# Activations stationary in the gated branch and the convolution input of an encoder trunk

## The chip, the cores and the metric

The kernel runs on one core of a Trainium2 chip. The metric is the device time of one execution in microseconds, the median of several runs. The engines named below are TensorE (PE; its weight loads are listed as PEld), VectorE (DVE), ScalarE (ACT), GpSimd (POOL) and the DMA queue of SyncE (SP). A matmul takes a stationary operand (128 x 128, loaded first) and streams a moving operand past it; the result goes to PSUM, whose banks hold 512 float32 columns on 128 partitions.

## What is computed

Two pre-norm residual layers over 256 tokens of width 2048 (float32). Layer 0 mixes tokens by neighbourhood attention, layer 1 by a gated short convolution; both end in a gated MLP with a convolution of three taps over the tokens, and a last norm closes the trunk.

```python
def short_conv_mixer(x, w_in, conv_w, w_out):
    gb, gc, h = jnp.split(x @ w_in, 3, axis=-1)          # 2048 -> 3 x 2048
    return (gb * dwconv_centered(gc * h, conv_w)) @ w_out

def conv_glu_ffn(x, w_up, conv_w, conv_b, w_down):       # 2048 -> 2 x 5632 -> 2048
    h = dwconv_centered(x @ w_up, conv_w) + conv_b
    g, u = jnp.split(h, 2, axis=-1)
    return (jax.nn.silu(g) * u) @ w_down

h = x
for i in range(2):
    a = rms_norm(h, mix_norm[i])
    h = h + (neighborhood_attention(a, ...) if i == 0 else short_conv_mixer(a, ...))
    h = h + conv_glu_ffn(rms_norm(h, ffn_norm[i]), ...)
return rms_norm(h, final_norm)
```

## The kernel before

Every float32 operand is split in two parts of the type fp32r, a rounded one (hi) and the rest (lo). A product is the sum of three: hi by hi, hi by lo, lo by hi. `split` and `scaled_split` do this for activations, `parts` for weights (ScalarE rounds, VectorE subtracts, L118 and L119).

Weights are streamed once, in chunks of 512 KB. `prep_to` loads them on the SP queue into `raw` (five buffers) and splits them into `hi` and `lo` (six each); it runs AHEAD = 4 chunks in front of the matmuls. Chunks of kind "rows" are one output tile by eight input tiles, 4 KB a partition; chunks of kind "cols" are four output tiles by two input tiles, four pieces of 1 KB a partition.

All work is a list `items`, one for each chunk, run in order by the loop at the end of `trunk`. What has to follow an item is put off with `after(n, fn)`: it is issued n items later. That list is the order of the program on every engine as far as the operands allow.

There are three kinds of product:

- **Phase** keeps a weight tile stationary and streams the activations (`a`, hi and lo side by side, 512 columns; then the lo weight against the hi activations, 256 columns, L156 and L157). Its result has channels on the partitions and tokens along the columns. `normed` adds the two halves and multiplies by `rstd` of each token, `conv` applies the taps to a padded tile in SBUF (L206 to L211), and the gate follows. Phase serves query and key (`wqk`), both halves of the gated branch (`wup`) and the convolution input (`wsc`).
- **Values** keeps the activations stationary (L474 to L476).
- **Tokens** keeps the activations stationary too, and streams the weights, 512 columns at a time, three matmuls for hi-hi, hi-lo and lo-hi (L304 to L306). Its result has tokens on the partitions, which the residual stream `h` needs. Two column blocks of 512 by two token tiles occupy the four `pm` banks. It serves the output projection, the down products and the convolution output. For the input pairs listed in `S_DOWN` and `S_OUT` the four blocks are computed by seven products instead of eight, from sums of blocks (`seven`, `sums`, `make_forms`), with four more banks (tags st, sc, tr, o).

A down half has 22 input tiles (11 pairs) and 2048 outputs; an up half has 44 output tiles. After each Tokens product that ends a mixer or an MLP, `to_norm` squares the new residual, transposes it back (L245) and scales it to the next `a`; `token_rstd` computes one over the root mean square, as a column `rcol` and spread over the partitions as `rstd` (L257).

Of the kernel before, what the change touches and what calls it, by code (L numbers as in the profile page):

```python
# [21 lines left out]
P = 128  # L23
# [11 lines left out]
CH = 8  # L35
AHEAD = 4

S_DOWN = (2, 5, 8)
S_OUT = (1, 3, 5)
# [12 lines left out]
def trunk(ctx, tc, xT, par, bias, wqk, wv, wo, wsc, wscout, wup, wdown, out):  # L52
# [12 lines left out]
    acc = cp.tile([P, S], F32, name="acc")  # L65
    NPAD = 3
    pads = [cp.tile([P, S + 2], F32, name=f"pad{i}") for i in range(NPAD)]
    pad_at = [0]

    def next_pad():  # L70
        pad_at[0] += 1
        return pads[pad_at[0] % NPAD]

# [7 lines left out]
    for p_ in pads:  # L81
        nc.gpsimd.memset(p_[:, 0:S + 2:S + 1], 0.0)
# [39 lines left out]
    def sums(l, r):  # L122

        t13 = wp.tile([P, CH * P], F32, name="raw", tag="raw", bufs=5)
# [70 lines left out]
    def normed(dst, ps):  # L195

        corr = tp.tile([P, S], F32, name="corr", tag="corr", bufs=3)
# [4 lines left out]
    def conv(x, w, b):  # L202

        c = tp.tile([P, S], F32, name="conv", tag="conv", bufs=4)
        if b is None:
            nc.scalar.activation(c, x[:, 1:S + 1], AF.Copy, scale=w[1])  # L206
        else:
            nc.scalar.activation(c, x[:, 1:S + 1], AF.Identity, scale=w[1], bias=b)  # L208
        for tap in (0, 2):
            nc.vector.scalar_tensor_tensor(out=c, in0=x[:, tap:tap + S], scalar=w[tap], in1=c,  # L210
                                           op0=ALU.mult, op1=ALU.add)  # L211
        return c
# [10 lines left out]
    def stats(sums):  # L223
# [4 lines left out]
        v = tp.tile([P, S], F32, name="v", tag="v", bufs=1)  # L228
        rt = tp.tile([P, 2, S], F32, name="rt", tag="s")
        rsqrt(rstd, v, rt[:, 0, :], rt[:, 1, :], ps)  # L230

    def residual(t, q, ps):
        x = h[:, t, q * 4 * P:(q + 1) * 4 * P]
        nc.vector.tensor_add(out=x, in0=ps, in1=x)

    def squares(t, q, ssq):
        nc.scalar.activation(tp.tile([P, 4 * P], F32, name="s", tag="s"), h[:, t, q * 4 * P:(q + 1) * 4 * P],
# [10 lines left out]
    def token_rstd(ssq):  # L248
# [3 lines left out]
        rsqrt(rcol, v, tp.tile([P, 2], F32, name="m", tag="m"), tp.tile([P, 2], F32, name="m", tag="m"), v)  # L252
        diag = tp.tile([P, S], F32, name="conv", tag="conv", bufs=4)
# [6 lines left out]
    class Tokens:  # L260
# [3 lines left out]
        def __init__(self, parts, src, evac, sset=(), forms=None):  # L264

            self.src, self.evac, self.sset, self.forms = src, evac, sset, forms
            self.nk = sum(n for _, n in parts)
            for g in range(KT // 8):
                base = 0
                for w, n in parts:  # L270
                    for k0 in range(0, n, 2):
                        k = base + k0
                        left, right = (w[f:f + 4, :, k0 * P:(k0 + 2) * P] for f in (8 * g, 8 * g + 4))
                        c = len(chunks)
                        chunks.append((left, 8 * P, "cols"))
                        if k // 2 in sset:
                            chunks.append((right, 8 * P, "sums"))
                            items.append((self, g, c + 1, k, k, k + 2))
                        else:
                            chunks.append((right, 8 * P, "cols"))  # L280
                            items.append((self, g, c, k, k, k + 2))
                            items.append((self, g, c + 1, k, k, k + 2))
                    base += n

        def run(self, g, c, k0, ka, kb):
            if k0 // 2 in self.sset:
                return self.seven(g, c, k0)
            hi, lo, _ = prepped[c]
            right = len(prepped[c - 1]) == 3 and (self, g, c - 1, k0, ka, kb) in items[at[0] - 1:at[0]]
            if not right and ka == 0:  # L290
                self.c = {n: pm.tile([P, 4 * P], F32, name="mm", tag="mm") for n in ("11", "21", "12", "22")}
                self.begun = set()
            for t in range(2):
                ps = self.c["12"[t] + "12"[right]]
# [5 lines left out]
                if kb == self.nk:  # L300
                    self.evac(t, 2 * g + right, ps)
# [6 lines left out]
        def seven(self, g, c, k0):  # L308
            i = k0 // 2
            first, last = i == min(self.sset), i == max(self.sset)  # L310
            if first:
                self.u = [pa.tile([P, 4 * P], F32, name="mu", tag=n) for n in ("st", "sc", "tr", "o")]
            a, e, f, b = self.u
# [4 lines left out]
            for ps, x, w, j in ((a, raw(0, 0), left, 0), (self.c["11"], raw(1, 0), left, 1), (self.c["12"], s4, w22, 0),  # L318
                                (e, s1, t13, 0), (f, s3, t13, 1), (b, s2, t24, 0), (self.c["21"], raw(1, 1), t24, 1)):
                own = ps in self.u  # L320
                self.product(ps, *x, *(y[:, j * 4 * P:(j + 1) * 4 * P] for y in w[:2]), own and first, own and last)
            if last:
                after(1, lambda: self.combine(g))

        def combine(self, g):

            a, e, f, b = self.u
            sa, u = (tp.tile([P, 4 * P], F32, name="s", tag="s") for _ in range(2))
            o = {(t, n): h[:, t, (2 * g + n) * 4 * P:(2 * g + n + 1) * 4 * P] for t in range(2) for n in range(2)}
# [8 lines left out]
            nc.vector.tensor_add(out=o[1, 0], in0=o[1, 0], in1=u)  # L338

    form_at = [0]  # L340

    def make_forms(xe, xo):

        n = form_at[0] = (form_at[0] + 1) % 3
        y = tp.tile([P, 8 * P], F32R, name="sf", tag="vv" if n else "sf", bufs=2 if n else 1)
        v = tp.tile([P, 4, P], F32, name="s", tag="s")
# [10 lines left out]
    def to_norm(n, a):  # L357
# [3 lines left out]
        def evac(t, q, ps):  # L361
            residual(t, q, ps)
            squares(t, q, ssq)

            def next_input():
                for k0, tag in zip(range(4 * q - 4, 4 * q + 4, 2), ("tr", "o", "sc", "st")):
                    tr = transposed(k0, tag)
                    for k in range(2):
                        a[k0 + k] = a_tile()
                        scaled_split(a[k0 + k], tr[:, k, :], norm_g(n, k0 + k))  # L370
            if t and q % 2:
                after(1, next_input)
                if q == KT // 4 - 1:
                    after(2, lambda: nc.vector.tensor_copy(rstd, token_rstd(ssq)))
        return evac
# [10 lines left out]
    def qk_evac(f, ps):  # L386
# [8 lines left out]
        if which == 0:  # L395
            b = tp.tile([P, 6 * GRID_W], F32, name="bias", tag="bias")
# [8 lines left out]
    def scores(h):  # L405
# [8 lines left out]
        s = tp.tile([P, 2, S], F32, name="s", tag="s")  # L414
# [80 lines left out]
    def sc_evac(f, ps):  # L495
        j, which = divmod(f, 3)
        w = [pt[:, C_SC + 3 * j + i:C_SC + 3 * j + i + 1] for i in range(3)]
        tag, bufs = ("conv", 4) if which else ("g", 2)
        t = tp.tile([P, S], F32, name="scx", tag=tag, bufs=bufs)
        normed(t, ps)  # L500
        if which == 0:
            sc_of["gc"] = t
        elif which == 1:
            pad = next_pad()
            nc.vector.tensor_mul(out=pad[:, 1:S + 1], in0=sc_of["gc"], in1=t)
            sc_of["c"] = conv(pad, w, None)
        else:
            nc.vector.tensor_mul(out=t, in0=t, in1=sc_of["c"])
            yT[j] = act_tile()
            split(yT[j], t)  # L510
            if j % 2 == 0:
                sc_of["even"] = t
            elif j // 2 in S_OUT:
                yforms[j // 2] = make_forms(sc_of["even"], t)
# [4 lines left out]
    def up_evac(layer, act, forms):  # L519
        def evac(f, ps):  # L520
            j, which = divmod(f, 2)
            ft = j + which * FT
            w = [pt[:, C_CW + (layer * 2 * FT + ft) * 3 + i:C_CW + (layer * 2 * FT + ft) * 3 + i + 1] for i in range(3)]
            b = pt[:, C_CB + layer * 2 * FT + ft:C_CB + layer * 2 * FT + ft + 1]
            pad = next_pad()
            normed(pad[:, 1:S + 1], ps)
            c = conv(pad, w, b)
            if which == 0:
                g = tp.tile([P, S], F32, name="g", tag="g")
                nc.scalar.activation(g, c, AF.Silu)  # L530
                glu["g"] = g
            else:
                nc.vector.tensor_mul(out=c, in0=c, in1=glu["g"])  # L533
# [4 lines left out]
                elif j % HALF // 2 in S_DOWN:  # L538
                    forms[j % HALF // 2] = make_forms(glu["even"], c)
# [3 lines left out]
    def last_evac():  # L543
# [3 lines left out]
        def evac(t, q, ps):  # L547
            residual(t, q, ps)
            squares(t, q, ssq)
# [159 lines left out]
```

## Time and profile before

| What | us |
|---|---|
| Median of 3 runs (2243.35 to 2248.56) | 2244.75 |
| The profiled execution's own time | 2248.17 |
| Its span, from the first instruction to the last | 2246.4 |
| VectorE busy | 1740.8 |
| ScalarE busy | 1216.9 |

The mean granted TensorE clock was 0.997 of full speed. Every group of lines is listed with its busy time and the mean duration of one instruction; for TensorE these durations overlap, so that the distance between starts, in the timeline, is what one costs. Idle time of an engine is listed with what ended it. The other lines stand in the prediction, where they are used.

### The profile page before, as it was taken

To read this page: it belongs to the slowest core of one execution; us is meant where nothing else is said; L and a number is where in the kernel's file an instruction comes from. 1 tells how busy PE (TensorE), PEld (TensorE's weight loads), DVE (VectorE), ACT (ScalarE), POOL (GpSimd) and SP (SyncE) were. 2 spreads that over 40 slices of the span, in tenths; PEclk is the share of its full clock that TensorE was granted. 3 is DMA by queue.
4 is the path that set the end of the run, shared out by engine and by line. 5 is a ranking of instruction groups with operands and counts; after the bars stand their busy time and mean duration, and the time that the engine had idled before them with its cause. 6 is when DMAs were issued, how large, how long until landed. Compare 5 with 4: busy or idle time off the path is not lost.

```text
span 2246.4 us, 31725 instructions
## 1 busy us (share of the span) xinstructions
PE 2226.4 (99%) x11818; PEld 1902.9 (85%) x11818; DVE 1740.8 (77%) x2546; ACT 1216.9 (54%) x1822; POOL 85.0 (4%) x110
## 2 busy tenths in 40 slices
PE   8999999999999999999999999999999999999997
PEld 6888888888888888888888888888888888888886
DVE  7777665687887778887877777898888778887876
ACT  5555554655554555555554444566555545555553
POOL 3111000000000000000000000000000000000000
PEclk9999999999999999999999999999999999999998
DMA  7565555555556655555665565565555666555563
GB/s 239 177 190 173 183 171 189 178 187 188 185 172 192 217 190 188 188 183 174 191 211 188 188 190 185 171 221 187 190 189 187 180 203 207 187 186 185 166 193 125
DMA packets 209689, 420.97 MB, mean 187 GB/s; under 512 B 13312, under 2 KB 136192, under 8 KB 209536
## 3 DMA queue, kind: packets, MB, share of 16 engines
q1 hardware_dynamic: 207792, 414.72, 58.0%
q0 software_dynamic: 1024, 3.15, 0.5%
q8 instruction: 93, 1.52, 0.3%
q10 hardware_dynamic: 720, 1.09, 0.1%
q14 instruction: 60, 0.49, 0.1%
HBM read 416.81 MB, written 2.10 MB: 186 GB/s over the span
## 4 chain that ended last, share of the span: by engine, by line
PE 98%; DVE 1%; issue 0%; ACT 0%; DVEq 0%
PE mm L156 42%; PE mm L157 21%; PE mm L304 8%; PE mm L306 8%; PE mm L305 8%; PE mm L474 1%; PE mm L475 1%; PE mm L476 1%; PE mu L305 1%; PE mu L304 1%; PE mu L306 1%; PE tr L245 1%; PE tr L436 0%; DVE a L573 0%; PE sc L412 0%
## 5 line engine op out<-in xcount | busy, mean ns | idle before, releaser
L156 PE MATMUL mm<-a,hi 128*128 128x512 f32 x4096 | 1445.3, 398 | 4.4 <-DVE a L186 3.2
L119 DVE TENSOR_TENSOR lo<-raw,hi 128x1024 fp32r<-128x1024 f32 (+1 forms) x820 | 988.8, 1213 | 392.6 <-ACT hi L118 388.7
L118 ACT CAST hi<-raw 128x1024 fp32r<-128x1024 f32 (+1 forms) x820 | 840.3, 1029 | 825.2 <-issue 465.0
L157 PE MATMUL mm<-a,lo 128*128 128x256 f32 x4096 | 1145.9, 280 | 0.8 <-DVE lo L119 0.8
L156 PEld LDWEIGHTS mm<-a,hi 128*128 128x128 f32 x4096 | 770.3, 188 | 192.3 <-DVE a L186 6.1
L157 PEld LDWEIGHTS mm<-a,lo 128*128 128x128 f32 x4096 | 773.7, 189 | 3.5 <-DVE lo L119 2.3
L304 PE MATMUL mm<-hi,act 128*128 128x512 f32 x780 | 304.6, 391 | 0.0
L306 PE MATMUL mm<-hi,act 128*128 128x512 f32 x780 | 304.1, 390 | 0.0
L305 PE MATMUL mm<-lo,act 128*128 128x512 f32 x780 | 303.5, 389 | 0.0
L210 DVE SCALAR_TENSOR_TENSOR conv<-pad,pt,conv 128x256 f32<-128x256 f32 x384 | 184.6, 481 | 10.9 <-ACT conv L208 3.9
L306 PEld LDWEIGHTS mm<-hi,act 128*128 128x128 f32 x780 | 146.4, 188 | 31.3
L305 PEld LDWEIGHTS mm<-lo,act 128*128 128x128 f32 x780 | 146.5, 188 | 30.5
L304 PEld LDWEIGHTS mm<-hi,act 128*128 128x128 f32 x780 | 146.4, 188 | 30.4
L208 ACT ACTIVATE conv<-pad,pt 128x256 f32<-128x256 f32 x176 | 105.4, 599 | 15.3 <-DVE pad L200 14.3
L199 DVE TENSOR_TENSOR corr<-mm,corr 128x256 f32<-128x256 f32 x256 | 106.4, 416 | 0.0
L198 ACT COPY corr<-mm 128x256 f32<-128x256 f32 x256 | 92.4, 362 | 0.4 <-PE mm L157 0.3
L200 DVE TENSOR_TENSOR pad<-corr,rstd 128x256 f32<-128x256 f32 x176 | 74.9, 426 | 5.6
L119 DVE TENSOR_TENSOR lo<-t,hi 128x1024 fp32r<-128x1024 f32 x30 | 36.7, 1224 | 22.9 <-ACT hi L118 22.8
L351 POOL TENSOR_TENSOR s<-conv 128x128 f32<-128x128 f32 x12 | 5.5, 461 | 1265.6 <-DVE conv L533 948.9
L474 PE MATMUL mm<-hi,a 128*128 128x512 f32 x128 | 50.7, 396 | 0.0
L118 ACT CAST hi<-t 128x1024 fp32r<-128x1024 f32 x30 | 31.5, 1049 | 35.3 <-PE mm L306 32.3
L475 PE MATMUL mm<-lo,a 128*128 128x512 f32 x128 | 49.9, 390 | 0.0
(140 smaller groups left out, 1300.2 us busy)
## 6 DMA issues: line engine op xcount, KB each, us to landing
raw<-in_wup SPq DMA_DIRECT2D x352, 512.0 KB, 4.0
raw<-in_wdown SPq DMA_DIRECT2D x176, 512.0 KB, 4.4
raw<-in_wsc SPq DMA_DIRECT2D x96, 512.0 KB, 4.3
raw<-in_wqk SPq DMA_DIRECT2D x58, 512.0 KB, 4.1
raw<-in_wv SPq DMA_DIRECT2D x32, 512.0 KB, 4.4
raw<-in_wo SPq DMA_DIRECT2D x32, 512.0 KB, 3.5
raw<-in_wscout SPq DMA_DIRECT2D x32, 512.0 KB, 4.4
raw<-in_wqk SPq DMA_DIRECT2D x12, 256.0 KB, 5.0
```

Source lines behind the costliest of these rows:

```text
L118: nc.scalar.copy(out=hv, in_=r)
L119: nc.vector.tensor_sub(out=lv, in0=r, in1=hv.bitcast(F32))
L156: nc.tensor.matmul(ps, lhsT=hi[:, o:o + P], rhs=x, start=k == 0, stop=False)
L157: nc.tensor.matmul(ps[:, S:], lhsT=lo[:, o:o + P], rhs=x[:, :S], start=False, stop=k == self.nk - 1)
L198: nc.scalar.copy(out=corr, in_=ps[:, S:])
L199: nc.vector.tensor_add(out=corr, in0=ps[:, :S], in1=corr)
L200: nc.vector.tensor_mul(out=dst, in0=corr, in1=rstd)
L208: nc.scalar.activation(c, x[:, 1:S + 1], AF.Identity, scale=w[1], bias=b)
L210: nc.vector.scalar_tensor_tensor(out=c, in0=x[:, tap:tap + S], scalar=w[tap], in1=c, op0=ALU.mult, op1=ALU.add)
L304: nc.tensor.matmul(ps, lhsT=xh, rhs=wh, start=start, stop=False)
L305: nc.tensor.matmul(ps, lhsT=xh, rhs=wl, start=False, stop=False)
L306: nc.tensor.matmul(ps, lhsT=xl, rhs=wh, start=False, stop=stop)
```

## The change

The gated branch (both halves, both layers) and the convolution input no longer run as Phase. A class `Product` takes the place of Tokens and serves them as well: activations stationary, weights moving, column groups of eight output tiles (a last narrow group of four where 44 doesn't divide), and weights in chunks of kind "cols". What becomes of a result is up to an `out` object. `Residual` is what Tokens did. `Branch` scales a block by `rcol` of each token on ScalarE while it copies it from PSUM, and transposes it on TensorE in pairs of output tiles, two to six items later; the taps then read the transposed tile in PSUM, and gate and split follow two items after. The taps write into columns 1 to 255 and 0 to 254, so the padded tiles go.

`S_UP` is empty: all products of the branch and of the convolution input are ordinary ones, and the `Branch.combine` and the "af" forms that the diff also adds are not run. `S_DOWN` and `S_OUT` become shorter by one pair each. `raw` has four buffers for five; the sum t13 moves out of them to the tag of t24. `rstd` is spread only for the end (and computed at the start for query and key, as before). Phase stays for query and key.

```diff
-S_DOWN = (2, 5, 8)
-S_OUT = (1, 3, 5)
+RAW = 4
+S_DOWN = (3, 6)
+S_OUT = (3, 5)
+S_UP = ()
...
-            raw = wp.tile([P, CH * P], F32, name="raw", tag="raw", bufs=5)
+            raw = wp.tile([P, CH * P], F32, name="raw", tag="raw", bufs=RAW)
...
-        t13 = wp.tile([P, CH * P], F32, name="raw", tag="raw", bufs=5)
+        t13 = tp.tile([P, CH * P], F32, name="t13", tag="qk")
...
-    def conv(x, w, b):
...
+    def taps(c, x, w):
+        nc.vector.scalar_tensor_tensor(out=c[:, 1:], in0=x[:, :S - 1], scalar=w[0], in1=c[:, 1:],
+                                       op0=ALU.mult, op1=ALU.add)
+        nc.vector.scalar_tensor_tensor(out=c[:, :S - 1], in0=x[:, 1:], scalar=w[2], in1=c[:, :S - 1],
+                                       op0=ALU.mult, op1=ALU.add)
...
-    class Tokens:
+    class Product:
+        def __init__(self, weights, cols, src, out, sset=(), forms=None):
+            self.src, self.out, self.forms = src, out, forms
+            self.nk = sum(n for _, n in weights)
+            f = cols[0]
+            while f < cols[1]:
+                wide = f + 8 <= cols[1]
+                own = tuple(sset) if wide else ()
...
+                        items.append((self, (f, own, 0), len(chunks) - 1, k, k, k + 2))
+                        if wide:
+                            chunks.append((right, 8 * P, "cols"))
+                            items.append((self, (f, own, 1), len(chunks) - 1, k, k, k + 2))
+                    base += n
+                f += 8 if wide else 4
...
+                    self.product(ps, xh, xl, wh, wl, k == 0, k == self.nk - 1)
                 if kb == self.nk:
-                    self.evac(t, 2 * g + right, ps)
+                    self.out.final(t, f // 4 + n, ps, self.part.get((t, n)))
+            if kb == self.nk:
+                self.out.done(f // 4 + n, n)
...
+    def quarter():
+        return tp.tile([P, 4 * P], F32, name="s", tag="s", bufs=4)
...
+    class Branch:
+        def final(self, t, q, ps, part):
+            if part is None:
+                part = quarter()
+                nc.scalar.activation(part, ps, AF.Copy, scale=rcol[:, t:t + 1])
...
+            self.x[t, q] = part
...
+        def done(self, q, n):
+            for i in range(2):
+                def pair(i=i):
+                    tr = pa.tile([P, 2, S], F32, name="tr", tag=BANKS[2 * n + i])
+                    for k in range(2):
+                        for t in range(2):
+                            nc.tensor.transpose(tr[:, k, t * P:(t + 1) * P],
+                                                self.x[t, q][:, (2 * i + k) * P:(2 * i + k + 1) * P], ident)
+                    self.evac(4 * q + 2 * i, tr)
+                after(2 * n + 2 + i, pair)
...
     def up_evac(layer, act, forms):
-        def evac(f, ps):
...
-            normed(pad[:, 1:S + 1], ps)
-            c = conv(pad, w, b)
...
+        def evac(f, tr):
+            j = f // 2
+            cs = []
+            for which in range(2):
...
+                c = tp.tile([P, S], F32, name="conv", tag="conv", bufs=4)
+                nc.scalar.activation(c, tr[:, which, :], AF.Identity, scale=pt[:, i + 1:i + 2], bias=pt[:, b:b + 1])
+                taps(c, tr[:, which, :], [pt[:, i + k:i + k + 1] for k in range(3)])
+                cs.append(c)
+
+            def gated():
+                gate, c = cs
+                nc.scalar.activation(gate, gate, AF.Silu)
+                nc.vector.tensor_mul(out=c, in0=c, in1=gate)
                 act[j % HALF] = act_tile()
                 split(act[j % HALF], c)
...
+            after(2, gated)
...
-            Phase(wup[layer], [f for j in range(lo, lo + HALF) for f in (2 * j, 2 * j + 1)], KT, a, up_evac(layer, act, forms),
-                  intro=0 if half else 3)
-            Tokens([(wdown[layer, half], HALF)], act, evac if half else residual, S_DOWN, forms)
+            Product([(wup[layer], KT)], (2 * half * HALF, 2 * (half + 1) * HALF), a,
+                    Branch(up_evac(layer, act, forms)), S_UP, aforms)
+            Product([(wdown[layer, half], HALF)], (0, KT), act, end if half else Residual(), S_DOWN, forms)
...
-    Phase(wsc, range(3 * KT), KT, a2, sc_evac, intro=3)
-    Tokens([(wscout, KT)], yT, to_norm(3, a3), S_OUT, yforms)
+    Product([(wsc, KT)], (0, 3 * KT), a2, Branch(sc_evac), S_UP, f2)
+    Product([(wscout, KT)], (0, KT), yT, to_norm(3, a3, S_UP, f3), S_OUT, yforms)
```

`sc_evac` changes in the same way: the first of its three columns is copied from PSUM by ScalarE, the second multiplied from PSUM by VectorE, and the third is copied and gated two items later.

More of the change, by code (lines that the diff above doesn't have):

```diff
@@ L64, in trunk @@
     rstd = cp.tile([P, S], F32, name="rstd")
[L65 to L72, printed above, removed]
     nc.vector.memset(ones, 1.0)
@@ L258, in token_rstd @@
         return bc
-    class Tokens:
[L264 to L268, printed above, removed]
+    BANKS = ("st", "sc", "tr", "o")
+    class Product:
[6 more added lines that the diff above has]
+                own = tuple(sset) if wide else ()
@@ L269, in __init__ @@
                 base = 0
-                for w, n in parts:
+                for w, n in weights:
                     for k0 in range(0, n, 2):
                         k = base + k0
-                        left, right = (w[f:f + 4, :, k0 * P:(k0 + 2) * P] for f in (8 * g, 8 * g + 4))
-                        c = len(chunks)
+                        left, right = (w[i:i + 4, :, k0 * P:(k0 + 2) * P] if i < cols[1] else None for i in (f, f + 4))
                         chunks.append((left, 8 * P, "cols"))
-                        if k // 2 in sset:
+                        if k // 2 in own:
@@ L283, in __init__, with run @@
                     base += n
-        def run(self, g, c, k0, ka, kb):
-            if k0 // 2 in self.sset:
-                return self.seven(g, c, k0)
+                f += 8 if wide else 4
+        def run(self, what, c, k0, ka, kb):
+            f, own, n = what
+            if n < 0:
+                return self.seven(f, own, c, k0)
             hi, lo, _ = prepped[c]
[L289 to L292, printed above, removed]
+            if n == 0 and ka == 0:
+                self.c, self.part = {}, {}
@@ L317, in seven, with combine, __init__ @@
             raw = lambda k, t: tuple(self.src[k0 + k][:, j + t * P:j + (t + 1) * P] for j in (0, S))
[L318 to L321, printed above, removed]
+            for ps, x, w, j in ((a, raw(0, 0), left, 0), (self.c[0, 0], raw(1, 0), left, 1), (self.c[0, 1], s4, w22, 0),
+                                (e, s1, t13, 0), (f_, s3, t13, 1), (b, s2, t24, 0), (self.c[1, 0], raw(1, 1), t24, 1)):
+                shared = ps in self.u
+                self.product(ps, *x, *(y[:, j * 4 * P:(j + 1) * 4 * P] for y in w[:2]), shared and first, shared and last)
             if last:
[L323 to L329, printed above, removed]
+                def combine():
+                    self.part = self.out.combine(f // 4, a, e, f_, b)
+                after(1, combine)
+    def quarter():
+        return tp.tile([P, 4 * P], F32, name="s", tag="s", bufs=4)
+    class Residual:
+        def __init__(self, then=None, ssq=None):
+            self.then, self.ssq = then, ssq
+        def final(self, t, q, ps, part):
+            x = h[:, t, q * 4 * P:(q + 1) * 4 * P]
+            nc.vector.tensor_add(out=x, in0=ps, in1=x)
+            if self.ssq is not None:
+                nc.scalar.activation(quarter(), x, AF.Square, accum_out=self.ssq[:, t, q:q + 1])
+        def combine(self, q, a, e, f, b):
+            sa, u = quarter(), quarter()
+            o = {(t, n): h[:, t, (q + n) * 4 * P:(q + n + 1) * 4 * P] for t in range(2) for n in range(2)}
             nc.scalar.copy(out=sa, in_=a)
@@ L493, in trunk, with sc_evac, sc_column @@
     sc_of = {}
-    def sc_evac(f, ps):
+    def sc_evac(f, tr):
+        for i in range(2):
+            sc_column(f + i, tr[:, i, :])
+    def sc_column(f, x):
         j, which = divmod(f, 3)
         w = [pt[:, C_SC + 3 * j + i:C_SC + 3 * j + i + 1] for i in range(3)]
-        tag, bufs = ("conv", 4) if which else ("g", 2)
-        t = tp.tile([P, S], F32, name="scx", tag=tag, bufs=bufs)
-        normed(t, ps)
         if which == 0:
-            sc_of["gc"] = t
+            t = sc_of["gc"] = tp.tile([P, S], F32, name="scx", tag="g")
+            nc.scalar.copy(out=t, in_=x)
@@ L503, in sc_evac @@
         elif which == 1:
-            pad = next_pad()
-            nc.vector.tensor_mul(out=pad[:, 1:S + 1], in0=sc_of["gc"], in1=t)
-            sc_of["c"] = conv(pad, w, None)
-        else:
[L508 to L514, printed above, removed]
+            v = tp.tile([P, S], F32, name="scx", tag="g")
@@ new lines, in sc_column, with gated @@
+            nc.vector.tensor_mul(out=v, in0=x, in1=sc_of["gc"])
+            c = sc_of["c"] = tp.tile([P, S], F32, name="conv", tag="conv", bufs=4)
+            nc.scalar.activation(c, v, AF.Copy, scale=w[1])
+            taps(c, v, w)
+        else:
+            t = tp.tile([P, S], F32, name="scx", tag="conv", bufs=4)
+            nc.scalar.copy(out=t, in_=x)
+            def gated(c=sc_of["c"]):
+                nc.vector.tensor_mul(out=t, in0=t, in1=c)
+                yT[j] = act_tile()
+                split(yT[j], t)
+                if j % 2 == 0:
+                    sc_of["even"] = t
+                elif j // 2 in S_OUT:
+                    yforms[j // 2] = make_forms(sc_of["even"], t, "vv")
+            after(2, gated)
@@ L517, in trunk @@
     glu = {}
     def up_evac(layer, act, forms):
-        def evac(f, ps):
[L521 to L525, printed above, removed]
-            normed(pad[:, 1:S + 1], ps)
-            c = conv(pad, w, b)
[L528 to L533, printed above, removed]
+        def evac(f, tr):
+            j = f // 2
+            cs = []
+            for which in range(2):
+                i = C_CW + (layer * 2 * FT + j + which * FT) * 3
+                b = C_CB + layer * 2 * FT + j + which * FT
+                c = tp.tile([P, S], F32, name="conv", tag="conv", bufs=4)
[6 more added lines that the diff above has]
+                nc.vector.tensor_mul(out=c, in0=c, in1=gate)
```

160 lines of the change are left out of this document (86 added, 74 removed).

## The prediction

> **What bounds the kernel now.** I read the page first: the share of each engine and the chain of work that ended last. In the chain's rows the percentages are shares of the span.
>
> ```profile
> span 2246.4 us, 31725 instructions
> ...
> PE 2226.4 (99%) x11818; PEld 1902.9 (85%) x11818; DVE 1740.8 (77%) x2546; ACT 1216.9 (54%) x1822; POOL 85.0 (4%) x110
> ...
> PE 98%; DVE 1%; issue 0%; ACT 0%; DVEq 0%
> PE mm L156 42%; PE mm L157 21%; PE mm L304 8%; PE mm L306 8%; PE mm L305 8%; PE mm L474 1%; PE mm L475 1%; PE mm L476 1%; PE mu L305 1%; PE mu L304 1%; PE mu L306 1%; PE tr L245 1%; PE tr L436 0%; DVE a L573 0%; PE sc L412 0%
> ```
>
> The chain is 98% TensorE, and 63% of it is the two matmuls of Phase (L156, L157). The next question is whether TensorE waits. In the view of waits, restricted to it, the columns are total us, times, longest us:
>
> ```profile
> PE st L257 <- DVE conv L255: 3.8, 1, 3.8
> PE mm L156 <- DVE a L186: 3.2, 5, 1.3
> PE mm L156 <- ACT hi L118: 1.2, 2, 0.9
> ```
>
> These are the three longest and come to 8 us. TensorE goes from one matmul to the next through the whole kernel. So the change is priced by counting TensorE's instructions and the distance from one start to the next. A matmul's busy time (some 390 ns) overlaps the next one and is no price. The view of windows, cut at the first matmul of each stage, gives the stages: up (first half, layer 0), down, up (second half), convolution input, its output product, and the two ups of layer 1. The row's second number is the stage's length.
>
> ```profile
> core 0: us, PE busy (x) PEld busy (x) DVE busy (x) ACT busy (x) POOL busy (x), PEclk, DMA share, GB/s
> ...
> 412.52:663.52 251.00, 251.00 (x1427) 217.84 (x1426) 203.27 (x326) 147.74 (x234) 8.33 (x12) 1.00 0.57 182
> 663.52:779.82 116.30, 116.30 (x512) 95.80 (x511) 90.72 (x107) 58.10 (x62) 0.00 (x0) 1.00 0.65 201
> 779.82:1028.55 248.73, 248.73 (x1409) 215.65 (x1408) 199.97 (x310) 140.29 (x219) 8.28 (x12) 1.00 0.57 185
> ...
> 1146.87:1415.68 268.81, 268.81 (x1556) 235.07 (x1554) 197.20 (x295) 131.53 (x191) 8.33 (x12) 1.00 0.58 188
> ...
> 1501.22:1747.74 246.52, 246.52 (x1427) 215.62 (x1426) 203.80 (x327) 146.19 (x233) 8.32 (x12) 1.00 0.58 187
> ...
> 1864.05:2112.78 248.73, 248.73 (x1409) 215.67 (x1408) 199.93 (x310) 140.23 (x219) 8.29 (x12) 1.00 0.58 185
> ```
>
> The five branch stages that change take 251.00 + 248.73 + 268.81 + 246.52 + 248.73 = 1263.8 us, at a granted clock of 1.00. An up half has 44 output tiles times 16 input tiles = 704 pairs of a 512-column and a 256-column matmul, so in the undisturbed second half a pair costs 248.73 / 704 = 353.3 ns.
>
> **Part 1: the products.** Per input tile and four output tiles, Phase issues 4 pairs (8 matmuls, 3072 columns). Product issues 2 token tiles times 3 products of 512 columns (6 matmuls, again 3072 columns). So only the distance per column matters. The branch has 4 x 704 + 768 = 3584 pairs; Product needs 3584 / 4 x 6 = 5376 matmuls of 512 columns. Their distance stands in the timeline of the output projection, which already runs with activations stationary, and in that of the values, which uses the same operands as the new branch (tile a stationary, hi and lo moving):
>
> ```profile
> 373.08 0.39 PE L304 MATMUL mm<-hi,act 128*128 128x512 f32 x1
> ...
> 381.92 0.39 PE L304 MATMUL mm<-hi,act 128*128 128x512 f32 x1
> ```
> ```profile
> 158.37 0.39 PE L474 MATMUL mm<-hi,a 128*128 128x512 f32 x1
> ...
> 162.22 0.39 PE L476 MATMUL mm<-hi,a 128*128 128x512 f32 x1
> ```
>
> The first fence spans 39 distances: 8.84 us / 39 = 226.7 ns. The second spans 17: 3.85 / 17 = 226.5 ns. I take 226.7. Then 5376 x 0.2267 = 1218.7 us. Per pair that is 340.1 ns where Phase needs 353.3, so the new shape itself is cheaper by 4%.
>
> A rule of the Trainium skill speaks against this term. TensorE: Matmul & The Clock Gate, section "Back-to-back issue gap", gives N/2.4 + 2.5 ns from start to start for N columns, that is 215.8 ns for 512 and 109.2 for 256. By it a pair would be 325.0 ns and Product's share 323.7, so the shape would save almost nothing and the sum below would be about 57 us instead of 18.8. The rows above, 226.7 ns for 512 columns and 353.3 per pair, agree with it for neither form.
>
> **Part 2: the transposes added.** Product leaves tokens on the partitions, so Branch.done transposes each 512-column block in two groups of four. There are 4 x 11 + 12 = 56 blocks, so 112 groups, 448 transposes. The values stage shows what such a group costs among matmuls:
>
> ```profile
> 162.90 0.39 PE L476 MATMUL mm<-hi,a 128*128 128x512 f32 x1
> 163.13 0.60 PE L436 MATMUL tr<-pt,s 128*128 128x128 f32 x4
> 163.49 0.47 PE L474 MATMUL mm<-hi,a 128*128 128x512 f32 x1
> 163.80 0.39 PE L475 MATMUL mm<-lo,a 128*128 128x512 f32 x1
> ...
> 165.41 0.39 PE L476 MATMUL mm<-hi,a 128*128 128x512 f32 x1
> ```
>
> From 162.90 to 165.41 are 2.51 us with nine matmuls in them. Nine at 226.5 ns are 2.04, so a group costs 0.472 us, its disturbed successors included (the next matmul follows after 0.31 instead of 0.23). 112 x 0.472 = 52.9 us. None of it is covered, because the engine they run on is the bound. The transposes of the residual, 16 in each of the three stages that begin after a norm, stay:
>
> ```profile
> 1089.65 1.75 PE tr L245 x16
> ...
> L436 PE MATMUL tr<-pt,s 128*128 128x128 f32 x64 | 9.6, 272 | 0.0
> ```
>
> The first row is of the chain in order of time, the second of the groups of lines (count, busy us and mean ns of one). With 3 x 1.75 = 5.3, the branch stages come to 1218.7 + 52.9 + 5.3 = 1276.9 us, or **13.1 us more** than 1263.8. (The small matmuls that spread rstd after three norms go; the windows before contain them, my sum after doesn't.)
>
> The same page of the Trainium skill, section "Part 4: PE-mode transpose", puts a 128x128 transpose at about 275 ns in a kernel and says that the clock is not released by transposes. This trace has the 275 as duration (272 ns) but not as distance: four take 0.36 us from 163.13 to 163.49, and PEclk stays at 1.00.
>
> **Part 3: fewer seven-product groups.** S_DOWN goes from three to two of eleven input pairs, S_OUT from three to two of eight. Each pair given up turns 21 matmuls into 24, in two column groups of each of five products: 48 ordinary for 42. The ordinary cost 0.2267; the down window gives the others: 116.30 = 384 x 0.2267 + 126 b, so b = 0.2321. 48 x 0.2267 - 42 x 0.2321 = 1.13 us, times five = **5.7 us**. The sum is 13.1 + 5.7 = **18.8 us**.
>
> **Part 4: what lies beside TensorE.** I cost it at nothing; these are the means behind that (busy us, mean ns, then idle before):
>
> ```profile
> L119 DVE TENSOR_TENSOR lo<-raw,hi 128x1024 fp32r<-128x1024 f32 x778 | 959.7, 1240 | 388.5 <-ACT hi L118 384.6
> L118 ACT CAST hi<-raw 128x1024 fp32r<-128x1024 f32 x778 | 814.6, 1051 | 805.3 <-issue 465.0 <-PE mm L306 207.5 <-PE mm L156 89.3
> ...
> L210 DVE SCALAR_TENSOR_TENSOR conv<-pad,pt,conv 128x256 f32<-128x256 f32 x384 | 184.6, 481 | 10.9 <-ACT conv L208 3.9 <-ACT conv L206 0.6
> ...
> L208 ACT ACTIVATE conv<-pad,pt 128x256 f32<-128x256 f32 x176 | 105.4, 599 | 15.3 <-DVE pad L200 14.3
> ...
> L182 DVE TENSOR_TENSOR act<-conv,act 128x256 fp32r<-128x256 f32 x88 | 39.8, 452 | 0.0
> L533 DVE TENSOR_TENSOR conv<-conv,g 128x256 f32<-128x256 f32 x88 | 37.3, 424 | 2.8
> ...
> L530 ACT ACTIVATE g<-conv 128x256 f32<-128x256 f32 x88 | 36.4, 413 | 9.6 <-DVE conv L210 9.6
> ...
> L181 ACT CAST act<-conv 128x256 fp32r<-128x256 f32 x88 | 35.3, 401 | 12.1 <-DVE conv L533 12.0
> ...
> L418 DVE SCALAR_TENSOR_TENSOR s<-sc,bias 128x256 f32<-128x256 f32 x32 | 12.1, 418 | 5.0 <-issue 3.1 <-PE sc L413 1.6
> ...
> L483 ACT ACTIVATE vv<-mm,rcol 128x512 fp32r<-128x512 f32 x8 | 5.5, 689 | 3.8 <-PE mm L476 3.8
> ```
>
> VectorE in an up half: 88 splits x 1.24 + 88 taps x 0.48 + 22 x (0.42 + 0.45) = 170 us of some 250, against 200 now, since the two additions of normed go. A tap that reads PSUM isn't in the trace; the nearest rows bound it at 0.418 (L418, one operand in PSUM) and 0.481 us (L210), and I take the dearer. ScalarE: 88 x 1.05 + 22 evacuations x 0.69 + 44 x 0.60 + 22 x (0.41 + 0.40) = 152 us, against 140. Both have a third of the stage free.
>
> The waits added sit well behind their causes. A block's accumulators are scaled by ScalarE right after the last product; the transposes follow two items later, and an item is 12 matmuls, 2.72 us, in which ScalarE has a cast (1.05) and two evacuations (1.38). Behind a waiting evacuation on ScalarE stand the casts of later weights, and VectorE's lo behind these. But weights are prepared four chunks ahead, 10.9 us of matmuls, so TensorE feels this only when that lead is gone. Each tr bank is asked for again 8 or 16 items later. In the down product that follows, the first seven-product group comes at item 6, while the last transposes (the half ends in a narrow group of four) come at item 2. The weights of up and convolution now come in the layout of down, and raw has four buffers for five:
>
> ```profile
> raw<-in_wup SPq DMA_DIRECT2D x352, 512.0 KB, 4.0
> raw<-in_wdown SPq DMA_DIRECT2D x176, 512.0 KB, 4.4
> ```
>
> 4.4 us from issue to landing, against three buffers ahead of the cast at 2.72 us each, 8.2 us. That hides it; the window of down shows the same layout at the same 226.7 ns pace with a DMA share of 0.65. On the SP queue one issue stands for one, and none moves past another.
>
> **The rivals.** (a) *Transposes at the column rate.* If a transpose cost 128/512 of 226.7 = 56.7 ns all told, the 448 would be 25.4 us for 52.9: 18.8 - 27.5 = -8.7, **2236 us**, faster. It decides below (52.9 - 18.8) / 448 = 76 ns each. For it: the 256-column matmul comes near its share of columns. Against: L436 shows 109 ns between them and a longer gap behind.
> (b) *The surplus of Phase belongs to the stage, not to the shape.* If what slows the pairs to 353 is the evacuation work beside them, the new matmuls inherit it: no saving, the branch stays at 1263.8 less 2 us of rstd matmuls, plus 52.9 and 5.7: +56.6, **2301 us**. For it: the pair varies between stages (246.52 - 1.75 in the first half of layer 1 is 347.7 per pair, 353.3 elsewhere). Against: the values' matmuls keep 226.5 next to such work. The rule of the Trainium skill on the issue gap would end near here too.
> (c) *The distance is that of the seven-product groups*, 232.1 for 226.7: 5376 x 0.0054 = 29.0 more, **2293 us**.
> (d) *TensorE waits for an evacuation* at every column group, with one scaling of 0.689 us: 30 groups x 0.69 = 20.7 more, **2284 us**. Against: the slack above.
> (e) *A transpose holds TensorE for its whole 272 ns*: 448 x 0.272 = 121.9 for 52.9, +87.8, **2333 us**. It is where the section on the PE-mode transpose in the Trainium skill would lead.
>
> **How the numbers follow.** The span would be 2246.4 + 18.8 = 2265.2 us. The profiled execution took 2248.17 us and the median of the runs is 2244.75, so I put the sum on the median: **2263.5 us**. Forecast 0.62 (itself 2250 to 2272; the part under 2249 is 0.03), (a) 0.09, (b) 0.10, (c) 0.09, (d) 0.08, (e) 0.02. From 2250 to 2294 are the forecast, (c) and (d), which leaves out about 2 in 10. A measurement of this kernel tells 0.2%, 4.5 us, from no change: faster 0.07 (most of a), same 0.05, slower 0.88.
>
> **What would show it.** Right: windows of 249 to 252 us for the up halves without the residual's transposes and near 274 for the convolution, 226 to 228 ns between products, 0.47 per group of four, VectorE near 170 us per half, down stages longer by 1.1. Wrong: waits of TensorE on ScalarE or VectorE at group borders (d), products at 232 or more (b, c), transposes under 76 ns (a).

## The result, and the profile after

The changed kernel takes 2272.49 us (median of 4 runs, 2270.07 to 2273.35), the kernel before 2244.05 us beside it (2243.22 to 2248.56): 1.0121 times as long, 95% interval 1.0103 to 1.0138, some 28 us slower. The profiled spans differ by 2270.5 - 2246.4 = 24.1 us.

The page of the changed kernel, cut to the lines that answer to those of before:

```profile
span 2270.5 us, 28384 instructions
...
PE 2246.7 (99%) x10498; PEld 1866.6 (82%) x10498; DVE 1502.2 (66%) x2024; ACT 1208.4 (53%) x1717; POOL 78.8 (3%) x87
...
PE 97%; DVE 1%; ACT 0%; DMA 0%; issue 0%; DVEq 0%; SPq 0%
PE mm L299 27%; PE mm L301 27%; PE mm L300 27%; PE mm L148 5%; PE mm L149 2%; PE tr L389 2%; PE mm L531 1%; PE mm L532 1%; PE mm L533 1%; PE mu L300 1%; PE mu L301 1%; PE mu L299 1%; PE tr L228 1%; DVE lo L111 0%; DMA act<-in_xT 0%
```

TensorE is still the whole chain. VectorE lost 239 us of busy time and ScalarE 9, and the kernel got slower: work off the chain was taken away, and work on it added. Its windows, cut at the first matmul of up (both halves of layer 0 with the down products between and behind), of the convolution input and of its output product:

```profile
core 0: us, PE busy (x) PEld busy (x) DVE busy (x) ACT busy (x) POOL busy (x), PEclk, DMA share, GB/s
416.38:667.42 251.04, 251.04 (x1153) 207.70 (x1152) 159.53 (x226) 144.12 (x206) 7.82 (x8) 1.00 0.60 184
667.42:785.82 118.40, 118.40 (x525) 97.69 (x524) 88.02 (x104) 57.22 (x63) 0.00 (x0) 1.00 0.65 195
785.82:1035.05 249.23, 249.23 (x1138) 206.05 (x1136) 155.28 (x212) 137.40 (x191) 7.85 (x8) 1.00 0.62 186
...
1155.27:1428.07 272.80, 272.80 (x1250) 225.68 (x1248) 151.07 (x179) 139.38 (x188) 5.85 (x8) 1.00 0.61 185
1428.07:1516.64 88.57, 88.57 (x406) 73.08 (x405) 76.39 (x102) 50.94 (x72) 0.00 (x0) 1.00 0.58 185
```

The undisturbed up half takes 249.23 us where it took 248.73: the cheaper products and the transposes nearly cancel there. The down product shown grows by 2.1 us: 1.1 are the shorter `S_DOWN`, and the rest is what the last two groups of transposes cost, which now stand in its window. One group in the up half, in the timeline of TensorE:

```profile
922.82 0.39 PE L301 MATMUL mm<-hi,a 128*128 128x512 f32 x1
923.05 0.60 PE L389 MATMUL tr<-pt,s 128*128 128x128 f32 x4
923.41 0.48 PE L299 MATMUL mm<-hi,a 128*128 128x512 f32 x1
923.72 0.40 PE L300 MATMUL mm<-lo,a 128*128 128x512 f32 x1
923.96 0.40 PE L301 MATMUL mm<-hi,a 128*128 128x512 f32 x1
924.19 0.40 PE L299 MATMUL mm<-hi,a 128*128 128x512 f32 x1
924.43 0.39 PE L300 MATMUL mm<-lo,a 128*128 128x512 f32 x1
...
925.81 0.39 PE L300 MATMUL mm<-lo,a 128*128 128x512 f32 x1
```

Four transposes take 0.36 us from start to start, the next matmul 0.31, and those behind it 0.23 to 0.24 instead of 0.227.

### The profile page after: what moved, and what is told of

Read it like the earlier page. It is cut to its first block, busy times and chain, and to the rows that moved or that the text cites. A ratio compares the mean times of both kernels' runs of the same rounds, so it can differ in the third digit from the quotient of the medians.

```text
span 2270.5 us, 28384 instructions
## 1 busy us (share of the span) xinstructions
PE 2246.7 (99%) x10498; PEld 1866.6 (82%) x10498; DVE 1502.2 (66%) x2024; ACT 1208.4 (53%) x1717; POOL 78.8 (3%) x87
## 4 chain that ended last, share of the span: by engine, by line
PE 97%; DVE 1%; ACT 0%; DMA 0%; issue 0%; DVEq 0%; SPq 0%
PE mm L299 27%; PE mm L301 27%; PE mm L300 27%; PE mm L148 5%; PE mm L149 2%; PE tr L389 2%; PE mm L531 1%; PE mm L532 1%; PE mm L533 1%; PE mu L300 1%; PE mu L301 1%; PE mu L299 1%; PE tr L228 1%; DVE lo L111 0%; DMA act<-in_xT 0%
## 5 line engine op out<-in xcount | busy, mean ns | idle before, releaser
L299 PE MATMUL mm<-hi,a 128*128 128x512 f32 x1792 | 708.5, 395 | 0.0
L301 PE MATMUL mm<-hi,a 128*128 128x512 f32 x1792 | 699.3, 390 | 0.0
L300 PE MATMUL mm<-lo,a 128*128 128x512 f32 x1792 | 697.6, 389 | 0.0
L301 PEld LDWEIGHTS mm<-hi,a 128*128 128x128 f32 x1792 | 336.4, 188 | 72.4
L300 PEld LDWEIGHTS mm<-lo,a 128*128 128x128 f32 x1792 | 336.9, 188 | 67.5
L299 PEld LDWEIGHTS mm<-hi,a 128*128 128x128 f32 x1792 | 336.6, 188 | 66.5
L148 PE MATMUL mm<-a,hi 128*128 128x512 f32 x512 | 187.7, 407 | 5.2 <-DVE a L178 4.2
L149 PE MATMUL mm<-a,lo 128*128 128x256 f32 x512 | 145.3, 285 | 1.0 <-DVE lo L111 1.0
L148 PEld LDWEIGHTS mm<-a,hi 128*128 128x128 f32 x512 | 98.1, 192 | 29.4 <-DVE a L178 5.7
L149 PEld LDWEIGHTS mm<-a,lo 128*128 128x128 f32 x512 | 98.7, 193 | 2.3 <-DVE lo L111 1.7
L593 ACT ACTIVATE conv<-tr,pt 128x256 f32<-128x256 f32 x176 | 94.5, 559 | 8.1 <-DVE conv L198 8.1
L196 DVE SCALAR_TENSOR_TENSOR conv<-tr,pt,conv 128x255 f32<-128x255 f32 x176 | 80.5, 476 | 2.8 <-ACT conv L593 2.8
L198 DVE SCALAR_TENSOR_TENSOR conv<-tr,pt,conv 128x255 f32<-128x255 f32 x176 | 80.6, 477 | 1.1
```

Source lines behind the costliest of these rows:

```text
L148: nc.tensor.matmul(ps, lhsT=hi[:, o:o + P], rhs=x, start=k == 0, stop=False)
L149: nc.tensor.matmul(ps[:, S:], lhsT=lo[:, o:o + P], rhs=x[:, :S], start=False, stop=k == self.nk - 1)
L196: nc.vector.scalar_tensor_tensor(out=c[:, 1:], in0=x[:, :S - 1], scalar=w[0], in1=c[:, 1:], op0=ALU.mult, op1=ALU.add)
L198: nc.vector.scalar_tensor_tensor(out=c[:, :S - 1], in0=x[:, 1:], scalar=w[2], in1=c[:, :S - 1], op0=ALU.mult, op1=ALU.add)
L299: nc.tensor.matmul(ps, lhsT=xh, rhs=wh, start=start, stop=False)
L300: nc.tensor.matmul(ps, lhsT=xh, rhs=wl, start=False, stop=False)
```

## The experiments

**The transposes.** One kernel leaves them out, another doubles them.

```diff
-                    tr = pa.tile([P, 2, S], F32, name="tr", tag=BANKS[2 * n + i])
-                    for k in range(2):
-                        for t in range(2):
-                            nc.tensor.transpose(...)
+                    tr = self.x[i, q].rearrange("p (k s) -> p k s", k=2)
```

> The changed kernel without the 448 transposes of the branch: the convolution reads the scaled block in SBUF as it lies, with tokens on the partitions. Forecast's theory (a group of four costs 0.472 us of TensorE and nothing hides it): 52.9 us less than the changed kernel's 2272.5, that is 2219.6 us, about 24 us under the kernel before. If transposes went at the column rate (rival a): 25 us less, 2247. If each held TensorE for its 272 ns (rival e): 122 us less, 2151. In the profile the product's distance should be 226.7 ns; if the 227.1 that the changed kernel shows in an up half is a surplus of the stage rather than of the transposes, it stays at 227.1.

Measured: 2217.31 us (2215.80 to 2217.95), 0.9872 of before (0.9857 to 0.9887), and a span of 2215.1. Its second up half in the windows:

```profile
774.35:1013.71 239.36, 239.36 (x1058) 198.26 (x1056) 156.37 (x212) 138.44 (x192) 9.36 (x8) 1.00 0.64 193
```

239.36 / 1056 = 226.7 ns for a product, to the digit what was forecast, and no surplus of the stage. The spans differ by 2270.5 - 2215.1 = 55.4 us, of which 0.6 arise ahead of the first up half (it begins at 415.76 us instead of 416.38). So the transposes cost 54.8 us, 0.489 per group instead of 0.472. The disturbance behind a group is longer here: ten distances, from 923.41 to 925.81 in the timeline above, average 0.240, and the eleventh is 0.227 again; in the rows from the values that the forecast used it is seven. What makes it longer stays open.

```diff
-                    for k in range(2):
+                    for k in (0, 1, 0, 1):
```

> Each group of four transposes of the branch is issued twice in a row, the second time over the same bank. Theory: 448 more at the distance of 109 ns inside a group, with no second disturbance behind it: 48.8 us more than the changed kernel, 2321 us. If part of the present transposes is hidden, the second set costs more than that (up to 53). If a transpose went at the column rate of 57 ns: 25 us more, 2298.

Measured: 2319.23 us, a span of 2317.1, so 46.6 us for 448 more, 104 ns each. Its second up half, where 249.23 us stood:

```profile
795.31:1052.81 257.50, 257.50 (x1218) 214.91 (x1216) 158.91 (x212) 137.62 (x191) 7.75 (x8) 1.00 0.59 180
```

The second set costs no more than the first, so nothing of the first was hidden, and rivals (a) and (e) are out: the price is neither 57 nor 272 ns.

**The surplus of Phase.** The kernel before, with the short matmul made long:

```diff
-                nc.tensor.matmul(ps[:, S:], lhsT=lo[:, o:o + P], rhs=x[:, :S], start=False,
-                                 stop=k == self.nk - 1)
+                nc.tensor.matmul(ps, lhsT=lo[:, o:o + P], rhs=x, start=False, stop=k == self.nk - 1)
```

> The kernel before, with the second matmul of Phase streaming all 512 columns of the activations instead of 256: it adds the product of the two low parts, so the weights stay stationary and the evacuation work beside the matmuls stays the same, and only the short matmul is gone. Theory (the surplus of Phase belongs to its shape, a weight load that has to fit under a 256-column matmul): every distance becomes 226.7 ns, 453.4 per pair, an up half takes 704 x 0.4534 = 319.2 us. Rival b (the surplus belongs to the stage): the pair keeps its 13 ns above the column rate or more, an up half takes 328 us or more.

The second up half in its windows:

```profile
900.74:1219.88 319.14, 319.14 (x1409) 264.26 (x1408) 201.74 (x312) 144.59 (x220) 5.94 (x12) 1.00 0.46 146
```

319.14 / 1408 = 226.7 ns, with weights stationary and the old evacuation beside it. The surplus belongs to the mixture of 512 and 256 columns; rival (b) falls. (The kernel as a whole takes 2665.78 us, for its longer matmuls.)

**The shorter sets**, alone, in the kernel before (`S_DOWN = (3, 6)`, `S_OUT = (3, 5)`):

> The kernel before with S_DOWN and S_OUT of the changed kernel, (3, 6) and (3, 5), and nothing else. Forecast's third part: 48 ordinary products for 42 in each of five stages, 1.13 us each, 5.7 us more than before: 2249.8 us. If the seven-product groups saved nothing here: no change. In the profile the down stages go from 116.3 to 117.4 us.

Measured: a span of 2252.1, 5.7 us above 2246.4, and in the windows

```profile
663.82:781.26 117.44, 117.44 (x518) 96.89 (x517) 85.03 (x99) 55.07 (x58) 0.00 (x0) 1.00 0.66 201
```

where 116.30 stood: 1.14 us, as worked out. The medians say more: 2262.00 us against 2252.51 for the kernel before beside it, a ratio of 1.0043 (1.0029 to 1.0056) or 6.5 to 12.6 us; the next run shows why medians of this kernel are worth less than its stages.

> The kernel before once more, for a second profile. The first profiled execution took 2248.2 us, the other runs about 2244. If the 4 us are a matter of the execution, this profile shows a span near 2242 and the place where it differs; if it is what the profiler costs, the span is 2246 again.

Measured: 2252.89 us, a span of 2251.1. The stages agree with the first profile within 0.1 us but for one, the convolution input:

```profile
1146.74:1420.45 273.71, 273.71 (x1556) 237.65 (x1554) 197.15 (x296) 131.57 (x191) 8.31 (x12) 1.00 0.58 185
```

It was 268.81. The same instructions at the same clock took 4.9 us longer. The timeline inside it, first in the first profile, then in this one:

```profile
1249.62 0.40 PE L156 MATMUL mm<-a,hi 128*128 128x512 f32 x1
...
1252.05 0.39 PE L156 MATMUL mm<-a,hi 128*128 128x512 f32 x1
```
```profile
1249.79 0.40 PE L156 MATMUL mm<-a,hi 128*128 128x512 f32 x1
...
1251.91 0.40 PE L156 MATMUL mm<-a,hi 128*128 128x512 f32 x1
```

Seven pairs in 2.43 us, 347 ns, against six in 2.12 us, 353 ns. Past its first hundred pairs, a stage holds one of two cadences. That is worth 4.5 to 4.9 us a stage (251.00 against 246.52, 273.71 against 268.81), and the kernel before was seen from 2242 to 2254.5 us in this study. The changed kernel has no such stage outside the attention, and its runs lie within 3.3 us.

**The attention**, which the prediction left out. The output projection begins at 324.54 us in place of 320.73, 3.8 later: 2.7 arise in the values stages, 1.1 in the first stage. In the changed kernel the bias shares buffers with the scores, so GpSimd loads and adds it later. One of the values stages (23.48 us before), a row of TensorE's waits, and the timeline at one of the delays:

```profile
74.93:99.44 24.51, 23.79 (x113) 19.52 (x111) 16.81 (x25) 11.63 (x19) 4.44 (x5) 1.00 0.64 205
```
```profile
PE sc L469 <- DVE qk L174: 1.7, 3, 0.7
```
```profile
154.53 2.25 DVE L111 TENSOR_TENSOR lo<-raw,hi 128x1024 fp32r<-128x1024 f32 x1 [0.84 <-ACT hi L110]
...
154.66 1.03 POOL L455 TENSOR_TENSOR bias<-bias,pt 128x384 f32<-128x384 f32 x1
...
156.71 0.41 DVE L174 TENSOR_TENSOR qk<-qk 128x256 fp32r<-128x256 f32 x1
...
157.17 0.39 PE L469 MATMUL sc<-qk 128*128 128x256 f32 x1 [0.48 <-DVE qk L174]
```

VectorE's split takes 2.25 us while GpSimd adds (1.23 elsewhere), the lo part of the key comes late, and the scores wait for it. The Trainium skill, SBUF — State Buffer, section "Terms", says of the port pair that the two engines share that the loser is blocked for the whole instruction; the trace agrees, 1.02 us lost beside an addition of 1.03.

```diff
-            b = tp.tile([P, 4 * P], F32, name="bias", tag="s", bufs=4)[:, :6 * GRID_W]
+            b = tp.tile([P, 6 * GRID_W], F32, name="bias", tag="bias")
```

> The changed kernel with the attention bias back in two buffers of its own, instead of the four that it shares with the scores and probabilities. Theory: the bias now waits for a transpose of an earlier head, so its transfer and addition on GpSimd come in the values stage and hold up VectorE's split there, and the scores wait for it: 1.0 + 0.75 + 0.75 us in three of four values stages. With its own buffers these stages return from 24.3 to 23.5 us: 2.5 us less, 2270. Rival: the smaller number of buffers for the corrections (two for three) does it; then the values stages stay at 24.3 and the time at 2272.5.

Measured: 2272.60 us, no gain. The values stages did return:

```profile
78.54:102.08 23.54, 23.54 (x113) 19.53 (x111) 16.33 (x25) 11.64 (x19) 2.66 (x3) 1.00 0.67 205
153.10:176.62 23.52, 23.52 (x113) 19.53 (x111) 15.22 (x22) 11.64 (x19) 1.92 (x2) 1.00 0.65 195
```

They were 24.51 and 24.26, and the waits of the scores are gone, so the shared buffer is their cause and the rival, the corrections' buffers, is not. But in the profiled execution the first stage, up to the first values, took 72.5 us instead of 69.2. That stage waits for the first transfers and varies: 68.0 to 69.7 in most profiles of this study, 72.2 to 73.0 in three kernels, one of them with the bias and the corrections in the buffers of before. What sets it stays open.

**Buffers of raw weights**: `RAW = 5`.

> The changed kernel with five raw buffers instead of four. Forecast's fourth part (4.2 us from issue to landing lie under 8.2 us of lead): no change beyond 1 us, 2272.5. If the shorter lead costs something anywhere, some us less.

Measured: 2272.51 us (2270.97 to 2272.82), stage by stage the same. A fifth buffer has nothing to hide.

**Two ways to a faster kernel.** The first uses what the change prepared, `S_UP = (3, 6)`, and the bias in its own buffers:

> The changed kernel with the bias in its own buffers and two input pairs (3 and 6 of eight) of the branch and the convolution input as seven-product groups. On TensorE each pair in each of the 26 wide column groups saves 24 x 0.2267 - 21 x 0.2321 = 0.57 us: 29.4 us less, with the bias 32 less, 2240.5 us, just under the kernel before. VectorE pays for it: per wide column group 12 splits x 1.24, two right chunks with sums of 5.9 us and two left of 1.24, 11.2 for taps, gate and split and 2.7 for the combination make 43 us in 44 us of TensorE. If VectorE or the quarter tiles become the bound there, TensorE waits and the time stays above 2250.

Measured: 2263.67 us, 1.0055 of before (1.0039 to 1.0070), a span 9.1 us under the changed kernel's instead of 32. With pair 6 as the last, the parts combined come one item after the left blocks were evacuated, so this kernel leaves their share out of two of the four blocks and saves VectorE a little work by it. Its second up halves, layer 0 and layer 1, TensorE's longest waits, and a stretch of the layer 1 half:

```profile
784.41:1031.14 246.73, 244.57 (x1107) 200.41 (x1106) 211.19 (x300) 159.92 (x225) 6.90 (x8) 1.00 0.61 187
1876.47:2125.72 249.25, 246.52 (x1108) 201.49 (x1107) 211.57 (x300) 159.89 (x225) 6.90 (x8) 0.99 0.60 184
```
```profile
PE mm L299 <- DVE s L367: 8.9, 7, 2.1
```
```profile
2016.88 0.50 PE L299 MATMUL mm<-hi,a 128*128 128x512 f32 x1 [2.09 <-DVE s L367]
...
2019.19 0.63 PE L301 MATMUL mm<-hi,a 128*128 128x512 f32 x1
2019.62 0.63 PE L299 MATMUL mm<-hi,a 128*128 128x512 f32 x1
2020.04 0.63 PE L300 MATMUL mm<-lo,a 128*128 128x512 f32 x1
```

VectorE goes from 155 to 211 us in a half, and TensorE waits for its evacuations. The saving of 5.7 us a half is reduced to 2.5 and to nothing. Waits are not all of it: these come to 8.9 of the 23 us that are missing. In the layer 1 half seven matmuls behind the longest wait stand 0.427 us apart instead of 0.227 (the granted clock there is 0.50), which takes some 1.6 of the 2.5 us between the two halves. The rest was not traced. A kernel with pairs 2 and 5, in which all parts would come early enough, gave no time, because its instructions wait for one another without end (a deadlock). So whether the late pair 6 has a share in the waits stays open.

The other follows from the cadences: the kernel before with its matmuls in another order.

```diff
+                for short in ((0, 1) if k % 2 == 0 else (1, 0)):
+                    if short:
+                        nc.tensor.matmul(ps[:, S:], lhsT=lo[:, o:o + P], rhs=x[:, :S], start=False, stop=False)
+                    else:
+                        nc.tensor.matmul(ps, lhsT=hi[:, o:o + P], rhs=x, start=k == 0, stop=k == self.nk - 1)
```

> The kernel before with the order of Phase's two matmuls turned round in every second input tile: 512, 256, 256, 512, 512, ... The same matmuls and operands. In three profiles of this shape the pairs hold one of two cadences for a whole stage, 346.7 or 353.3 ns, against 340.0 for 768 columns at 226.7 per 512. Theory (the surplus comes at the change between a long and a short matmul, whose weights are loaded under the short one): a pair costs 340 to 347 in every stage. Of the five branch stages and those of query and key 4096 pairs gain between 0 and 13.3 ns: 2205 to 2240 us. Rival (each load under a 256-column matmul pays, wherever it stands): 346.7 to 353.3 as before, 2244 to 2253.

Measured: 2240.53 us (2239.45 to 2241.45), 0.9968 of before (0.9956 to 0.9979), which took 2247.90 beside it. Convolution input and a second up half in its windows:

```profile
1139.56:1409.50 269.94, 269.94 (x1555) 235.55 (x1554) 198.44 (x295) 134.57 (x191) 11.01 (x12) 1.00 0.59 187
1860.09:2105.32 245.23, 245.23 (x1410) 213.97 (x1409) 202.30 (x312) 146.54 (x220) 11.27 (x12) 1.00 0.59 187
```

245.23 / 704 = 348.3 ns, and past the first hundred pairs the same in every branch stage: one cadence in place of two, between the rival's bounds. The time lies in neither range: half a microsecond above the theory's 2205 to 2240, 3.5 below the rival's 2244 to 2253.

> The kernel before with Phase's matmuls of a chunk in two runs: the eight (in the first tiles four) 512-column ones, then the 256-column ones. The same matmuls and operands. Theory (the surplus comes at the change between long and short): two changes a chunk instead of sixteen, near 340.5 ns a pair in every stage, 4096 pairs gain 6 to 13 ns: 2195 to 2225 us. Rival (a load under a 256-column matmul always pays): the 256-column ones stand 117 to 127 ns apart and the time stays at 2244 to 2253.

Measured: 2243.96 us, 0.9989 (0.9978 to 0.9999). In the timeline of its convolution input:

```profile
1250.00 2.00 PE L161 MATMUL mm<-a,hi 128*128 128x512 f32 x8
1251.84 1.12 PE L158 MATMUL mm<-a,lo 128*128 128x256 f32 x8
1252.79 2.00 PE L161 MATMUL mm<-a,hi 128*128 128x512 f32 x8
```

With two changes a chunk in place of sixteen a pair still takes (1.84 + 0.95) / 8 = 349 ns, so the theory of the changes falls. The eight short ones take 119 ns each for the 113 that 226.7 would make, as the rival has it. But the rival is not the whole: the eight long ones take 230 ns each, more than the 226.7 of streams without short ones. Both kinds stand further apart where they share a stream; what causes it stays open.

## Why the prediction came out as it did

The time, 2272.49, lies in the range and the sign was right; the sum was 18.8 us where the spans show 24.1 and the medians 28.4. The time is half a microsecond above the forecast's own band, 2250 to 2272, and lies in the range thanks to the room left for rivals (c) and (d), neither of which occurred. In that much the hit is luck. By its steps:

- **Part 1, the products**: right. Without transposes the five branch stages take 241.17 + 239.36 + 262.94 + 241.17 + 239.36 = 1224.0 us, 39.8 less than before; the forecast had 1218.7 + 5.3 = 1224.0. Two readings beside it were wrong. The fast pairs of 347 ns are not in the first half of layer 1 alone: the convolution input has them too, (268.81 - 1.75) / 768 = 347.7. The total of 1263.8 holds even so. And the rule on the issue gap, set against this part, would make the sum about 52 us and not 57, an estimate, since by its figures a pair still gets 1.3 ns cheaper. The 226.7 ns contradict it here. The Trainium skill, TensorE: Matmul & The Clock Gate, section "Back-to-back issue gap", gives that rule for a single matmul by itself, which the prediction left out.
- **Part 2, the transposes**: right in mechanism, 1.9 us short. 54.8 against 52.9, with more matmuls disturbed behind a group than in the quoted row.
- **Part 3, the shorter sets**: 5.7 us forecast, 5.7 measured alone.
- **Part 4, nothing else**: right for the branch. From 416 us to the end products TensorE shows no wait at all, so rival (d) did not occur; VectorE's half took 155 us, even less than 170. It failed for the attention: the shared buffers there were not looked at, and they (2.7 us) and the first stage (1.1) cost 3.8 us.
- **The sum put on the median**: the step that cost most, by a little. -39.8 + 54.8 + 5.7 + 3.8 = 24.5, about the 24.1 of the spans. But the profiled execution of before, at 2248.17, lay 4.1 us above the median of 2244.05, and the changed kernel has no such spread. The second profile shows a spread of that size from the cadence of one stage; that a cadence made this difference too was not seen, since no execution at 2244 was profiled.

Rivals (a), (b) and (e) are refuted by runs, and (c), products at 232 ns, by the 226.7.

## What to carry to other kernels

Where one engine is the whole chain, count its instructions by their distance in the neighbourhood in which they will run; a busy share or a rule for a single matmul would have missed both terms here. Taking a seventh of VectorE's busy time away (239 of 1741 us) bought nothing, and each group of transposes put on the bound was paid in full (0.489 us, 54.8 in all), with the disturbance behind it. Before a sum is put on a median, look whether the kernel before has stages that run in more than one way.

## What was not expected of the hardware

A stream of alternating 512- and 256-column matmuls, each with new weights, ran at 346.7 or at 353.3 ns a pair, constant through a stage past its first hundred pairs; the same stage of the same kernel did either. Streams of 512 columns alone held 226.7 ns, away from transposes and outside the seven-product groups (232). What chooses the cadence was not found. Turning the order round in every second tile gives 348.3 in all branch stages, and with 2240.53 us the fastest of the kernels here that do the whole computation.
